# Turning the memory-gate rows by transfers through DRAM instead of TensorE transposes

## The chip, the cores and the metric

The kernel runs on one core of a Trainium2 chip. The metric is the device time of one execution in microseconds. The kernel before took 701.46 us in the median of three runs (700.98 to 701.46).

## The reference, cut to what matters

One layer of a streaming encoder, 512 tokens of 1024 channels, in float32. The normalised input goes through one wide projection (11,272 columns) that feeds two token mixers and two merge gates; the mixers' outputs are projected, merged, projected again and added to the input. The part that the change touches is the first mixer, a matrix memory with 4 heads. Two rows per head, an input gate and a forget gate, steer it:

```python
log_i = mi.transpose(0, 2, 1)                    # (B, heads, tokens)
log_f = jax.nn.log_sigmoid(mf).transpose(0, 2, 1)
bcum  = jnp.cumsum(fb, axis=-1)                  # per chunk
dmat  = bcum[..., :, None] - bcum[..., None, :] + ib[..., None, :]
m_t   = jnp.maximum(inter, jnp.max(dmat, axis=-1))
w_intra = jnp.exp(dmat - m_t[..., None])
h = num / jnp.maximum(jnp.abs(den), jnp.exp(-m_t))[..., None]
```

So every weight between a token t and an earlier token s is the exponential of (something of t) plus (something of s). The kernel works these out as a row over t, `rb`, and a column over s, `c`, with blocks of 128 tokens. Rows lie along one partition's free axis, columns along the partitions, and the numbers have to be had both ways.

## The kernel before, in words

The whole layer is a list of 110 units, numbered c. A unit is one block of weights (512 KB) with its 24 matmuls of 512 columns on TensorE (PE): each product is made three times, from a high and a low part of both operands (L85, L86, L87; the first four units have L1137 to L1139). A unit's weights are loaded by SP into one of three buffers `stg` (L110), split into `wh` on ScalarE (L90) and `wl` on VectorE (L91) up to two units ahead (AHEAD), and loaded up to four units ahead (LOADS); since there are three buffers, the load of the weights of one unit waits until the split three units earlier is through.

Beside the units run generators. The loop over c calls each active generator once per unit (not in the units in REST: 11, 16, 20, ...), and a `yield` ends its share of that unit. Instructions stand in each engine's queue in this order and engines work their queues in order, so what a generator issues in unit c stands behind the split for unit c+2 and ahead of that for unit c+3. The attention heads (from unit 10 on) send their blocks `ay` to `az` by 16 transfers per head on SP, in two halves (L458), and split `az` on ScalarE and VectorE a few units later. The four memory heads start in units 52, 56, 70 and 76.

The gates are one generator that starts in unit 4. The 4 heads' forget gates come out of TensorE as rows on partitions 32 to 35 (`g2`), the input gates on 0 to 3. Four transposes turn the forget rows into columns `f` of 128 partitions by 16 numbers (L546), where log-sigmoid is worked out; four transposes turn them back into rows (L570); two scans along the rows give `m` and `b` (L575, L581); `rb`, `c` and a copy of `rb` in two parts, `rb2`, follow (L583 to L587). Eight transposes and a product with ones then give `c_lag[0]`, `em` and `bs` as columns (L600 to L607), and `c_lag[1..3]` follow from them (L610). A memory head spreads its row of `rb` over the 128 partitions by one product with a selector `sel` (L706) and a copy out of the PSUM (L708); POOL masks the diagonal blocks into `w_all` (L713), and ScalarE takes the exponentials with `c_lag` as bias (L724).

Of the kernel before, what the change touches and what calls it, by code (L numbers as in the profile page):

```python
# [8 lines left out]
F32 = mybir.dt.float32  # L9
FR = mybir.dt.float32r  # L10
BF = mybir.dt.bfloat16
AF = mybir.ActivationFunctionType
OP = mybir.AluOpType

D = 1024
T = 512
KT = 8
TB = 4
# [16 lines left out]
def tile_hybrid_layer(  # L35
# [16 lines left out]
    nc = tc.nc  # L52
# [3 lines left out]
    def pool(name, bufs=1, **k):  # L56
        return ctx.enter_context(tc.tile_pool(name=name, bufs=bufs, **k))

    cst = pool("cst")
    hp = pool("hp")  # L60
    sp = pool("sp")
    mp = pool("mp")
    tiny = pool("tiny", 4)
    psd = pool("psd", 4, space=bass.MemoryType.PSUM)
    psa = pool("psa", 4, space=bass.MemoryType.PSUM)
    ctx.enter_context(tc.manual_schedule())
# [6 lines left out]
    def blk(tag, dt=F32, shape=(512,), name=None, p=128):  # L73

        where = mp if tag in MISC else sp
        return where.tile([p] + list(shape), dt, name=name or tag, tag=tag, bufs=BUFS[tag])
# [4 lines left out]
    def att_ps():  # L81
        return psa.tile([128, 512], F32, name="aps", tag="aps")
# [128 lines left out]
    ident = cst.tile([128, 128], F32, name="ident")  # L211
# [282 lines left out]


    NH = 4
    sel = cst.tile([128, NH, 128], FR, name="sel")
    rb2 = cst.tile([128, T], FR, name="rb2")
    c_lag = [cst.tile([128, TB, NH], F32, name=f"c_lag{k}") for k in range(TB)]
    em = cst.tile([128, TB, NH], F32, name="em")  # L500
    gst = blk("y", shape=(KT, 8), name="gst")

    wg_t = []

    def gates_fill():
        wg = blk("P5", FR, (KT, 128), name="wg")
        nc.gpsimd.memset(wg.bitcast(F32), 0.0)

        sel32 = blk("y", shape=(NH, 128), name="sel32", p=36)
        nc.gpsimd.memset(sel32, 1.0)  # L510
        for r in (slice(0, 4), slice(32, 36)):
            nc.gpsimd.affine_select(out=sel32[r], in_=sel32[r], compare_op=OP.is_equal, fill=0.0, base=0,
                                    channel_multiplier=1, pattern=[[-1, 4], [0, 128]])
        nc.gpsimd.memset(sel.bitcast(F32), 0.0)
        nc.gpsimd.memset(rb2.bitcast(F32), 0.0)
        wg_t.extend([wg, sel32])

    def gates_prep():
        wg, sel32 = wg_t
        for c in range(2):  # L520
            src = gst[:, :, 4 * c:4 * c + 4]
            nc.vector.tensor_copy(wg[:, :, 32 * c:32 * c + 4], src)
            nc.vector.tensor_tensor(wg[:, :, 64 + 32 * c:68 + 32 * c], src,
                                    wg[:, :, 32 * c:32 * c + 4].bitcast(F32), op=OP.subtract)
        nc.vector.tensor_copy(sel[0:4], sel32[0:4])
        nc.vector.tensor_copy(sel[32:36], sel32[32:36])

    def gates():
        def row(name, p=4):
            return blk("y", name=name, p=p)  # L530

        wg = wg_t[0]
        ps = att_ps()
        for k in range(KT):
            nc.tensor.matmul(ps, wg[:, k, :], hh[:, k, :], start=k == 0, stop=False)
            nc.tensor.matmul(ps, wg[:, k, :], hl[:, k, :], start=False, stop=k == KT - 1)
        g1 = row("g1", 36)
        nc.scalar.activation(g1, ps[64:100, :], AF.Copy)
        g2 = row("g2", 36)
        nc.vector.scalar_tensor_tensor(g2, ps[0:36, :], gbias, g1, op0=OP.add, op1=OP.add)  # L540
        gi = g2[0:4, :]
        yield

        fp = att_ps()
        for j in range(TB):
            nc.tensor.transpose(fp[:, 4 * j:4 * j + 4], g2[32:36, j * 128:(j + 1) * 128], ident[32:36, 32:36])  # L546

        def col(name):
            return tiny.tile([128, 16], F32, name=name, bufs=1)

        f, u, w, p = col("gf"), col("gu"), col("gw"), col("gp")
        nc.vector.tensor_copy(f, fp[:, 0:16])
        nc.scalar.activation(u, f, AF.Abs)
        nc.scalar.activation(u, u, AF.Exp, scale=-1.0)
        nc.scalar.activation(w, u, AF.Sigmoid)
        yield
        nc.vector.tensor_scalar(w, u, 2.0, None, op0=OP.add)
        nc.vector.reciprocal(w, w)
        nc.vector.tensor_tensor(u, u, w, op=OP.mult)
        nc.vector.tensor_tensor(w, u, u, op=OP.mult)  # L560
        nc.vector.tensor_scalar(p, w, 2.0 / 17, 2.0 / 15, op0=OP.mult, op1=OP.add)
        for c in (13, 11, 9, 7, 5, 3, 1):
            nc.vector.tensor_tensor(p, p, w, op=OP.mult)
            nc.vector.tensor_scalar(p, p, 2.0 / c, None, op0=OP.add)
        nc.vector.tensor_tensor(u, u, p, op=OP.mult)
        nc.vector.scalar_tensor_tensor(f, f, 0.0, u, op0=OP.min, op1=OP.subtract)
        yield
        lp = att_ps()
        for j in range(TB):
            nc.tensor.transpose(lp[0:4, j * 128:(j + 1) * 128], f[:, 4 * j:4 * j + 4], ident)  # L570
        f = row("gl")
        nc.vector.tensor_copy(f, lp[0:4, :])
        yield
        m = row("gm")
        nc.vector.tensor_tensor_scan(m, f, gi, 0.0, op0=OP.add, op1=OP.max)  # L575
        msk = row("gk")
        nc.vector.memset(msk, 1.0)
        nc.vector.memset(msk.rearrange("p (b t) -> p b t", b=TB)[:, :, 0:1], 0.0)
        b = row("gp")
        nc.vector.tensor_tensor_scan(b, msk, f, 0.0, op0=OP.mult, op1=OP.add)  # L580
        yield  # L581
        rb = row("gu")
        nc.vector.tensor_tensor(rb, b, m, op=OP.subtract)  # L583
        nc.vector.tensor_copy(rb2[0:4], rb)
        nc.vector.tensor_tensor(rb2[32:36], rb, rb2[0:4].bitcast(F32), op=OP.subtract)
        c = row("gw")
        nc.vector.tensor_tensor(c, gi, b, op=OP.subtract)  # L587
        ones4 = row("ones4")
        bend = ones4[:, 128:144].rearrange("p (x h) -> p x h", h=NH)
        ones4 = ones4[:, 0:128]  # L590
        for h in range(NH):
            nc.vector.tensor_scalar(bend[:, :, h:h + 1],
                                    b.rearrange("p (x t) -> p x t", x=TB)[:, :, 127:128],
                                    ident[0:4, h:h + 1], None, op0=OP.mult)
        nc.vector.memset(ones4, 1.0)
        yield
        tp = att_ps()
        for j in range(TB):
            js = slice(j * 128, (j + 1) * 128)
            nc.tensor.transpose(tp[:, 4 * j:4 * j + 4], c[:, js], ident[0:4, 0:4])  # L600
            nc.tensor.transpose(tp[:, 16 + 4 * j:20 + 4 * j], m[:, js], ident[0:4, 0:4])
        bb = att_ps()
        nc.tensor.matmul(bb[:, 0:16], ones4, bend.rearrange("p x h -> p (x h)"), start=True, stop=True)
        nc.vector.tensor_copy(c_lag[0], tp[:, 0:16].rearrange("p (j h) -> p j h", h=NH))
        nc.vector.tensor_copy(em, tp[:, 16:32].rearrange("p (j h) -> p j h", h=NH))
        bs = cst.tile([128, TB, NH], F32, name="bs")
        nc.vector.tensor_copy(bs, bb[:, 0:16].rearrange("p (j h) -> p j h", h=NH))  # L607
        for k in range(1, TB):
            n = TB - k
            nc.vector.tensor_tensor(c_lag[k][:, 0:n, :], c_lag[k - 1][:, 0:n, :],  # L610
                                    bs[:, k - 1:k - 1 + n, :], op=OP.add)
# [4 lines left out]
    class MPair:  # L616
# [84 lines left out]
        def head(self, h):  # L701
            hd = 2 * self.p + h
            qt = self.tr["q"][2 * h:2 * h + 2]
            kt = self.tr["k"][2 * h:2 * h + 2]
            rp = att_ps()
            nc.tensor.matmul(rp, sel[:, hd, :], rb2, start=True, stop=True)  # L706
            rbc = blk("om", shape=(516,))
            nc.vector.tensor_copy(rbc[:, 0:T], rp)  # L708
            w_all = blk("P5", shape=(1280,), name="w_all")
            for j in range(TB):  # L710
                lo = j * 128
# [2 lines left out]
                                        fill=-1e30, base=0, channel_multiplier=-1, pattern=[[1, 128]])  # L714
# [3 lines left out]
            for j in range(TB):  # L718
                lo = j * 128
                w = w_all[:, P_OFF[j]:P_OFF[j] + T - lo]  # L720
                for i in range(j, TB):
                    s = slice((i - j) * 128, (i - j + 1) * 128)
                    src = w[:, s] if i == j else rbc[:, i * 128:(i + 1) * 128]
# [74 lines left out]
            src = ht.rearrange("p (d a) i j -> p a d (i j)", d=2)  # L798
# [6 lines left out]
            for d in range(2):  # L805
                y = y_m[2 * hd + d].rearrange("p (i b j) -> p i b j", i=TB, b=4)
# [337 lines left out]

    later.setdefault(3, []).append(turn_vecs)
    later.setdefault(GATES_PREP, []).append(gates_prep)


    act = []
    pend = [(GATES_START, 1, lambda: True, gates)]  # L1150
    for s in (0, 1):
        for h in range(4):
# [30 lines left out]
    for c in range(N):  # L1183
# [17 lines left out]
        if c == 0:  # L1201
            x_scale(2)
            x_scale(3)
            gates_fill()
# [45 lines left out]
```

## Time and profile before

| | |
|---|---|
| median of three runs | 701.46 us (700.98 to 701.46) |
| the profiled execution's own time | 700.42 us |
| its span | 698.7 us |
| PE busy | 690.4 us, 99% |
| VectorE (DVE), ScalarE (ACT), GpSimd (POOL) busy | 463.5, 335.6, 109.2 us |
| mean busy share of the DMA engines, per 40th of the span | between 2 and 7 tenths |
| granted TensorE clock | full in every slice |

The span is what the trace covers; the execution's own time is 1.72 us longer. PE is the engine that is always at work, and the chain that ended last lies on it for 97% of the span. A busy PE says little by itself, since matmuls overlap and their ends are modelled; what a group of matmuls takes is read here from the starts of those around it. In steady stretches of 512-column products the starts lie 0.22 to 0.23 us apart.

### The profile page before, as it was taken

The page shows a single profiled execution, that of the slowest core. Times are in us where ns is not written, and L with a number is a line of the kernel's source. Part 1 is how long each engine was busy: PE and PEld are TensorE (multiplying, and loading weights), DVE is VectorE, ACT ScalarE, POOL GpSimd, SP SyncE. Part 2 cuts the span into 40 slices and gives each one's busy share as a digit, 9 for nine tenths or more (in the row PEclk, how much of TensorE's full clock was granted, in tenths as well). Part 3 has the DMA queues.
Part 4 walks back from the last instruction along what each step waited for, and adds up shares of the span by engine and source line. Part 5 has one row for each costly group of instructions (what it writes and reads, how often), then busy time and mean ns, then how long its engine had stood idle before and what let it go on. Part 6 is the DMA issues. An engine that isn't in the chain of part 4 may idle for free.

```text
span 698.7 us, 9267 instructions
## 1 busy us (share of the span) xinstructions
PE 690.4 (99%) x3220; PEld 575.2 (82%) x3220; DVE 463.5 (66%) x807; ACT 335.6 (48%) x629; POOL 109.2 (16%) x249
## 2 busy tenths in 40 slices
PE   7999999999999999999999999999999999999997
PEld 5888888888888888888888888888888888888876
DVE  6837887856787775389944738995343364445996
ACT  6245354475554543244475534446563353344451
POOL 5422122252130220000011120001111000111021
PEclk9999999999999999999999999999999999999999
DMA  7432424525433444333332244433323456589434
GB/s 247 136 106 71 126 63 123 148 59 145 112 107 84 130 109 137 90 95 94 97 98 67 61 108 120 120 90 91 91 61 86 112 157 219 144 184 208 126 81 130
DMA packets 104759, 80.94 MB, mean 116 GB/s; under 512 B 6766, under 2 KB 89096, under 8 KB 104712
## 3 DMA queue, kind: packets, MB, share of 16 engines
q1 hardware_dynamic: 102552, 74.45, 37.2%
q0 software_dynamic: 2016, 5.77, 4.5%
q8 instruction: 25, 0.41, 0.2%
q14 instruction: 22, 0.18, 0.1%
q10 hardware_dynamic: 144, 0.13, 0.1%
HBM read 65.12 MB, written 2.10 MB: 96 GB/s over the span
## 4 chain that ended last, share of the span: by engine, by line
PE 97%; DMA 1%; DVE 1%; POOL 0%; SPq 0%; issue 0%; ACT 0%; DVEq 0%
PE dps L85 27%; PE dps L86 27%; PE dps L87 27%; PE aps L86 3%; PE aps L87 3%; PE aps L85 3%; PE aps L389 1%; PE dps L1139 1%; PE dps L1137 1%; PE dps L1138 1%; DMA stg<-in_w_in_dram 1%; PE aps L760 1%; PE aps L762 1%; PE aps L761 1%; DVE fl L1096 0%; POOL fl L1096 0%
## 5 line engine op out<-in xcount | busy, mean ns | idle before, releaser
L91 DVE TENSOR_TENSOR wl<-stg,wh 128x1024 fp32r<-128x1024 f32 x92 | 112.6, 1223 | 112.9 <-ACT wh L90 111.3
L85 PE MATMUL dps<-hh,wh 128*128 128x512 f32 x448 | 175.2, 391 | 0.0
L87 PE MATMUL dps<-hh,wl 128*128 128x512 f32 x448 | 174.5, 389 | 0.0
L86 PE MATMUL dps<-hl,wh 128*128 128x512 f32 x448 | 174.5, 389 | 0.0
L90 ACT ACTIVATE wh<-stg 128x1024 fp32r<-128x1024 f32 x92 | 96.8, 1052 | 58.4 <-PE dps L87 38.2
L87 PEld LDWEIGHTS dps<-hh,wl 128*128 128x128 f32 x448 | 84.1, 188 | 17.8
L85 PEld LDWEIGHTS dps<-hh,wh 128*128 128x128 f32 x448 | 84.1, 188 | 17.1 <-DVE tmp L372 0.4
L86 PEld LDWEIGHTS dps<-hl,wh 128*128 128x128 f32 x448 | 84.2, 188 | 16.9
L85 PE MATMUL dps<-wh,hh 128*128 128x512 f32 x224 | 88.2, 394 | 0.1
L87 PE MATMUL dps<-wh,hl 128*128 128x512 f32 x224 | 87.3, 390 | 0.0
L86 PE MATMUL dps<-wl,hh 128*128 128x512 f32 x224 | 87.3, 390 | 0.0
L87 PEld LDWEIGHTS dps<-wh,hl 128*128 128x128 f32 x224 | 42.0, 188 | 9.0
L85 PEld LDWEIGHTS dps<-wh,hh 128*128 128x128 f32 x224 | 42.1, 188 | 8.6 <-issue 0.5
L86 PEld LDWEIGHTS dps<-wl,hh 128*128 128x128 f32 x224 | 42.1, 188 | 8.1
L651 DVE SCALAR_TENSOR_TENSOR acc<-tmp,vec,acc 128x511 f32<-128x511 f32 (+2 forms) x48 | 36.0, 750 | 1.7
L654 ACT ACTIVATE tmp<-acc 128x512 f32<-128x512 f32 x16 | 10.1, 633 | 50.8 <-DVE acc L651 50.8
L422 DVE TENSOR_TENSOR_SCAN om<-om 128x512 f32<-128x512 f32 (+3 forms) x32 | 26.7, 835 | 8.8 <-POOL om L416 8.8
L416 POOL TENSOR_SCALAR_AFFINE_SELECT om<-om 128x128 f32<-128x128 f32 x32 | 14.1, 441 | 109.0 <-ACT om L414 109.0
L713 POOL TENSOR_SCALAR_AFFINE_SELECT w_all<-om 128x128 f32<-128x128 f32 x16 | 6.0, 412 | 153.9 <-DVE om L708 136.8
L414 ACT ACTIVATE om<-aps,rq 128x512 f32<-128x512 f32 (+3 forms) x32 | 16.8, 525 | 22.8 <-PE aps L87 22.8
L85 PE MATMUL dps<-yh,wh 128*128 128x512 f32 x64 | 24.9, 389 | 0.0
L86 PE MATMUL dps<-yl,wh 128*128 128x512 f32 x64 | 24.9, 389 | 0.0
(271 smaller groups left out, 1225.3 us busy)
## 6 DMA issues: line engine op xcount, KB each, us to landing
stg<-in_w_in_dram SPq DMA_DIRECT2D x87, 512.0 KB, 3.8
az<-ay SPq DMA_DIRECT2D x128, 40.0 KB, 2.0
stg<-in_w_proj_s_dram SPq DMA_DIRECT2D x8, 512.0 KB, 3.7
B<-in_w_out_dram SPq DMA_DIRECT2D x8, 512.0 KB, 4.8
stg<-in_w_proj_m_dram SPq DMA_DIRECT2D x8, 512.0 KB, 3.6
wl<-stg POOLq DMA_DIRECT2D x8, 512.0 KB, 5.5
brow<-in_b_in_dram SPq DMA_DIRECT2D x8, 256.0 KB, 4.0
hz<-ht SPq DMA_DIRECT2D x64, 32.0 KB, 1.9
```

Source lines behind the costliest of these rows:

```text
L85: nc.tensor.matmul(ps, ah, bh, start=first, stop=False)
L86: nc.tensor.matmul(ps, ah, bl, start=False, stop=False)
L87: nc.tensor.matmul(ps, al, bh, start=False, stop=last)
L90: nc.scalar.activation(hi, src, AF.Copy)
L91: nc.vector.tensor_tensor(lo, src, hi.bitcast(F32), op=OP.subtract)
L389: nc.tensor.transpose(tp[:, tb * 128:(tb + 1) * 128], self.raw[name][tb][:, hs], ident)
L414: nc.scalar.activation(om[:, 0:n], zp, AF.Sigmoid, scale=rn[:, h:h + 1])
L416: nc.gpsimd.affine_select(out=om[:, ts], in_=om[:, ts], compare_op=OP.is_gt, fill=1.0, base=0, channel_multiplier=1, pattern=[[-1, 128]])
L422: nc.vector.tensor_tensor_scan(back, back, back, 1.0, op0=OP.mult, op1=OP.bypass)
L651: nc.vector.scalar_tensor_tensor(acc[:, j:], t[:, 0:T - j], cw(3 - j, ch), acc[:, j:], op0=OP.mult, op1=OP.add)
L654: nc.scalar.activation(t, acc, AF.Sigmoid)
L760: nc.tensor.matmul(nm[:, 0:258], ph, vh, start=j == 0, stop=False)
```

## The change

The transposes, the selector products and their PSUM copies go. In their place rows and columns are written to small DRAM tensors (`f_d`, `l_d`, `rb_d`, `c_d`, `m_d`, `b_d`: 8 KB each) and read back in the other order by transfers on SP. The new helper `by_token` reads a (4, 512) tensor back as 128 partitions by 4 numbers, 128 tokens at a time; each number is 4 bytes and its neighbours in the tile lie 2 KB apart in DRAM. A memory head reads its row of `rb_d` on all 128 partitions at once. The generator has four more `yield`s.

```diff
 def gates_fill():
-        sel32 = blk("y", shape=(NH, 128), name="sel32", p=36)
-        ... (memsets and selects of sel32, sel, rb2 on POOL)
 def gates_prep():
-        nc.vector.tensor_copy(sel[0:4], sel32[0:4])
-        nc.vector.tensor_copy(sel[32:36], sel32[32:36])
 def gates():
+        def by_token(dst, src):
+            for j in range(TB):
+                nc.sync.dma_start(dst[:, 4 * j:4 * j + 4],
+                                  src[:, j * 128:(j + 1) * 128].rearrange("h p -> p h"))
...
-        fp = att_ps()
-        for j in range(TB):
-            nc.tensor.transpose(fp[:, 4 * j:4 * j + 4], g2[32:36, j * 128:(j + 1) * 128], ident[32:36, 32:36])
-        nc.vector.tensor_copy(f, fp[:, 0:16])
+        f_d = dp.tile([NH, T], F32, name="f_d")
+        nc.sync.dma_start(f_d, g2[32:36, :])
+        yield
+        by_token(f, f_d)
+        yield
+        yield
...
-        lp = att_ps()
+        l_d = dp.tile([128, 16], F32, name="l_d")
+        nc.sync.dma_start(l_d, f)
+        yield
+        f = row("gl")
         for j in range(TB):
-            nc.tensor.transpose(lp[0:4, j * 128:(j + 1) * 128], f[:, 4 * j:4 * j + 4], ident)
-        f = row("gl")
-        nc.vector.tensor_copy(f, lp[0:4, :])
+            nc.sync.dma_start(f[:, j * 128:(j + 1) * 128], l_d[:, 4 * j:4 * j + 4].rearrange("p h -> h p"))
+        yield
         yield
...
-        nc.vector.tensor_copy(rb2[0:4], rb)
-        nc.vector.tensor_tensor(rb2[32:36], rb, rb2[0:4].bitcast(F32), op=OP.subtract)
+        nc.sync.dma_start(rb_d, rb)
...
-        (ones4 and bend: four products by ident's columns, a memset)
+        c_d, m_d, b_d = [dp.tile([NH, T], F32, name=n) for n in ("c_d", "m_d", "b_d")]
+        for d, src in ((c_d, c), (m_d, m), (b_d, b)):
+            nc.sync.dma_start(d, src)
         yield
-        tp = att_ps()
+        by_token(c_lag[0].rearrange("p j h -> p (j h)"), c_d)
+        by_token(em.rearrange("p j h -> p (j h)"), m_d)
+        bs = cst.tile([128, TB, NH], F32, name="bs")
         for j in range(TB):
-            nc.tensor.transpose(tp[:, 4 * j:4 * j + 4], c[:, js], ident[0:4, 0:4])
-            nc.tensor.transpose(tp[:, 16 + 4 * j:20 + 4 * j], m[:, js], ident[0:4, 0:4])
-        bb = att_ps()
-        nc.tensor.matmul(bb[:, 0:16], ones4, bend.rearrange("p x h -> p (x h)"), start=True, stop=True)
-        (three copies out of the PSUM)
+            nc.sync.dma_start(bs[:, j, :], bass.AP(tensor=b_d.tensor, offset=b_d.offset + 128 * j + 127,
+                                                   ap=[[0, 128], [T, NH]]))
+        yield
+        yield
...
 class MPair, def head(self, h):
-            rp = att_ps()
-            nc.tensor.matmul(rp, sel[:, hd, :], rb2, start=True, stop=True)
             rbc = blk("om", shape=(516,))
-            nc.vector.tensor_copy(rbc[:, 0:T], rp)
+            nc.sync.dma_start(rbc[:, 0:T], bass.AP(tensor=rb_d.tensor, offset=rb_d.offset + T * hd,
+                                                   ap=[[0, 128], [1, T]]))
```

On PE, where the first attention head's transposes (`qraw`, `kraw`) begin in unit 10, this stood before:

```order
L87 MATMUL dps<-wh,hl 128x512
L600 MATMUL aps<-ident,gw 128x4
L601 MATMUL aps<-ident,gm 128x4
L600 MATMUL aps<-ident,gw 128x4
L601 MATMUL aps<-ident,gm 128x4
L600 MATMUL aps<-ident,gw 128x4
L601 MATMUL aps<-ident,gm 128x4
L600 MATMUL aps<-ident,gw 128x4
L601 MATMUL aps<-ident,gm 128x4
L603 MATMUL aps<-ones_781 128x16
L389 MATMUL aps<-ident,qraw 128x128 x4
```

and this stands there now (the line numbers are one higher):

```order
L86 MATMUL dps<-wh,hh 128x512
L87 MATMUL dps<-wl,hh 128x512
L88 MATMUL dps<-wh,hl 128x512
L390 MATMUL aps<-ident,qraw 128x128 x4
L390 MATMUL aps<-ident,kraw 128x128 x4
```

The nine rows of the gates are gone. The four transposes of L546, the four of L570 and the four selector products of L706 leave PE's queue in the same way, and nothing else in it moves.

On SP, in the stretch of units 9 to 18, this stood before (`stg` are the weight loads, `brow` a bias row, `az` the attention heads' blocks):

```order
L110 DMA stg<-in_w_in_dram 128x8x128 x2
L304 DMA brow<-in_b_in_dram 128x512
L110 DMA stg<-in_w_in_dram 128x8x128 x2
L110 DMA stg<-in_w_in_dram 128x2x512 x4
L458 DMA az<-ay 32x320 x8
L110 DMA stg<-in_w_in_dram 128x2x512 x2
L458 DMA az<-ay 32x320 x8
L304 DMA brow<-in_b_in_dram 128x512
```

and from the second of these rows on this stands there now (`gl` are the turned forget rows, `c_lag`, `em` and `bs` the columns):

```order
L305 DMA brow<-in_b_in_dram 128x512
L111 DMA stg<-in_w_in_dram 128x8x128
L566 DMA l_d<-gf 128x16
L111 DMA stg<-in_w_in_dram 128x8x128
L111 DMA stg<-in_w_in_dram 128x2x512
L570 DMA gl<-l_d 4x128x1 x4
L111 DMA stg<-in_w_in_dram 128x2x512 x3
L583 DMA rb_d<-gu 4x512
L588 DMA c_d<-gw 4x512
L588 DMA m_d<-gm 4x512
L588 DMA b_d<-gp 4x512
L459 DMA az<-ay 32x320 x8
```

```order
L111 DMA stg<-in_w_in_dram 128x2x512 x2
L525 DMA c_lag_101<-c_d 128x4x1 x4
L525 DMA em<-m_d 128x4x1 x4
L594 DMA bs<-b_d 128x4x1 x4
L459 DMA az<-ay 32x320 x8
L305 DMA brow<-in_b_in_dram 128x512
```

The first half of the first head's `az` has moved behind four writes that wait for `gu` and `gw` of VectorE, and the second half behind twelve transfers of single numbers.

On VectorE the rows' scans leave the stretch of units 6 to 10 and stand now in unit 14 (in front of the attention head's `ay`), with `gu` and `gw` one unit on:

```order
L92 TENSOR_TENSOR wl<-stg,wh 128x1024
L574 SCALAR_TENSOR_TENSOR gm<-gl,g_508 4x512
L576 MEMSET gk 4x512
L577 MEMSET gk 4x4
L579 SCALAR_TENSOR_TENSOR gp<-gk,gl 4x512
L441 STREAM_TRANSPOSE ay<-a_all 128x4x32 x5
```

Before, the same scans stood behind the copy of `gl` out of the PSUM; now the first of them waits for four transfers.

## Rows read from the trace of the kernel before

**Rows 1.** The page's chain that ended last: shares of the span by engine.

```profile
PE 97%; DMA 1%; DVE 1%; POOL 0%; SPq 0%; issue 0%; ACT 0%; DVEq 0%
```

**Rows 2.** One stretch: length, busy PE, PEld, DVE, ACT, POOL, clock, DMA share, GB/s.

```profile
36.60:660.00 623.40, 623.34 (x2930) 522.51 (x2929) 404.25 (x700) 301.87 (x565) 85.80 (x210) 1.00 0.42 113
```

**Rows 3.** Timeline of PE around L546 and L570: start us, duration us, line.

```profile
48.41 0.39 PE L87 MATMUL dps<-wh,hl 128*128 128x512 f32 x1
...
49.41 0.40 PE L86 MATMUL dps<-wl,hh 128*128 128x512 f32 x1
...
59.85 0.39 PE L87 MATMUL dps<-wh,hl 128*128 128x512 f32 x1
...
60.75 0.39 PE L86 MATMUL dps<-wl,hh 128*128 128x512 f32 x1
```

**Rows 4.** Timeline of PE around L600 to L603, and at the second attention head.

```profile
76.64 0.39 PE L87 MATMUL dps<-wh,hl 128*128 128x512 f32 x1
...
77.78 0.33 PE L389 MATMUL aps<-ident,qraw 128*128 128x128 f32 x1
...
96.80 0.34 PE L87 MATMUL aps<-kth,qtl 128*128 128x384 f32 x1
96.97 0.60 PE L389 MATMUL aps<-ident,qraw 128*128 128x128 f32 x4
```

**Rows 5.** Timeline of PE at two of the four selector products.

```profile
350.61 0.39 PE L706 MATMUL aps<-rb,sel 128*128 128x512 f32 x1
350.84 0.40 PE L85 MATMUL dps<-hh,wh 128*128 128x512 f32 x1
...
370.96 0.44 PE L706 MATMUL aps<-rb,sel 128*128 128x512 f32 x1
371.24 0.40 PE L85 MATMUL dps<-hh,wh 128*128 128x512 f32 x1
```

**Rows 6.** Timeline of SP: issues in units 12 to 18, and in unit 52.

```profile
84.01 0.37 SPq L110 DMA_DIRECT2D stg<-in_w_in_dram  x1
...
116.97 5.28 SPq L458 DMA_DIRECT2D az<-ay  x8
...
122.98 0.37 SPq L110 DMA_DIRECT2D stg<-in_w_in_dram  x1
...
341.23 0.37 SPq L110 DMA_DIRECT2D stg<-in_w_in_dram  x1
```

**Rows 7.** Timelines of DVE, ACT and PE in the same units.

```profile
102.47 1.23 DVE L91 TENSOR_TENSOR wl<-stg,wh 128x1024 fp32r<-128x1024 f32 x1
...
109.30 1.22 DVE L91 TENSOR_TENSOR wl<-stg,wh 128x1024 fp32r<-128x1024 f32 x1 [0.20 <-ACT wh L90]
...
354.00 0.68 DVE L708 COPY om<-aps 128x512 f32<-128x512 f32 x1
...
133.77 1.03 ACT L90 ACTIVATE ath<-az 128x512 fp32r<-128x512 f32 x2
...
142.40 1.04 ACT L90 ACTIVATE wh<-stg 128x1024 fp32r<-128x1024 f32 x1
...
119.77 0.39 PE L85 MATMUL dps<-wh,hh 128*128 128x512 f32 x1
```

**Rows 8.** The page's DMA issues: KB each, median us to landing.

```profile
stg<-in_w_in_dram SPq DMA_DIRECT2D x87, 512.0 KB, 3.8
az<-ay SPq DMA_DIRECT2D x128, 40.0 KB, 2.0
...
brow<-in_b_in_dram SPq DMA_DIRECT2D x8, 256.0 KB, 4.0
```

**Rows 9.** The first 16 us by stretch, columns as in rows 2.

```profile
13.00:14.40 1.40, 1.30 (x10) 1.13 (x10) 1.40 (x2) 1.15 (x2) 1.40 (x2) 1.00 0.83 168
10.00:13.00 3.00, 2.09 (x10) 1.38 (x8) 2.46 (x8) 2.77 (x6) 2.54 (x5) 1.00 1.05 416
14.40:16.00 1.60, 1.24 (x5) 0.48 (x3) 1.60 (x2) 1.15 (x2) 1.52 (x2) 1.00 0.03 6
```

More of the change, by code (lines that the diff above doesn't have):

```diff
@@ L63, in tile_hybrid_layer @@
     tiny = pool("tiny", 4)
+    dp = pool("dp", space=bass.MemoryType.DRAM)
     psd = pool("psd", 4, space=bass.MemoryType.PSUM)
@@ L496, in tile_hybrid_layer @@
     NH = 4
-    sel = cst.tile([128, NH, 128], FR, name="sel")
-    rb2 = cst.tile([128, T], FR, name="rb2")
+    rb_d = dp.tile([NH, T], F32, name="rb_d")
     c_lag = [cst.tile([128, TB, NH], F32, name=f"c_lag{k}") for k in range(TB)]
@@ L507, in gates_fill @@
         nc.gpsimd.memset(wg.bitcast(F32), 0.0)
-        sel32 = blk("y", shape=(NH, 128), name="sel32", p=36)
[L510 to L516, printed above, removed]
+        wg_t.append(wg)
     def gates_prep():
-        wg, sel32 = wg_t
+        wg = wg_t[0]
         for c in range(2):
@@ L583, in gates @@
         nc.vector.tensor_tensor(rb, b, m, op=OP.subtract)
-        nc.vector.tensor_copy(rb2[0:4], rb)
-        nc.vector.tensor_tensor(rb2[32:36], rb, rb2[0:4].bitcast(F32), op=OP.subtract)
+        nc.sync.dma_start(rb_d, rb)
         c = row("gw")
         nc.vector.tensor_tensor(c, gi, b, op=OP.subtract)
[L588 to L595, printed above, removed]
+        c_d, m_d, b_d = [dp.tile([NH, T], F32, name=n) for n in ("c_d", "m_d", "b_d")]
+        for d, src in ((c_d, c), (m_d, m), (b_d, b)):
+            nc.sync.dma_start(d, src)
         yield
-        tp = att_ps()
+        by_token(c_lag[0].rearrange("p j h -> p (j h)"), c_d)
+        by_token(em.rearrange("p j h -> p (j h)"), m_d)
+        bs = cst.tile([128, TB, NH], F32, name="bs")
         for j in range(TB):
-            js = slice(j * 128, (j + 1) * 128)
-            nc.tensor.transpose(tp[:, 4 * j:4 * j + 4], c[:, js], ident[0:4, 0:4])
-            nc.tensor.transpose(tp[:, 16 + 4 * j:20 + 4 * j], m[:, js], ident[0:4, 0:4])
-        bb = att_ps()
-        nc.tensor.matmul(bb[:, 0:16], ones4, bend.rearrange("p x h -> p (x h)"), start=True, stop=True)
[L604 to L607, printed above, removed]
+            nc.sync.dma_start(bs[:, j, :], bass.AP(tensor=b_d.tensor, offset=b_d.offset + 128 * j + 127,
+                                                   ap=[[0, 128], [T, NH]]))
+        yield
+        yield
         for k in range(1, TB):
```

## The prediction, made before the changed kernel ran

> **What bounds the kernel now.** I read the chain of waits first: it lies on PE for 97% of the span [rows 1]. Then the busy times by stretch: from 36.60 to 660.00 us PE is at work in 623.34 of 623.40 us, with the clock granted in full (1.00, the 2.4 GHz level), while VectorE and ScalarE are busy for 404 and 302 us and the DMA engines for a mean of 0.42 [rows 2]. All the gate work and all four memory heads lie in that stretch. So a PE instruction taken out there ends everything behind it earlier by what it took of PE's queue, unless PE then waits; and a transfer or a VectorE operation put in or taken out is worth nothing until it makes PE wait. Two questions are left: what the removed PE instructions took, and whether the added transfers are late for anyone whom PE waits for.
>
> **What is removed from PE.** Matmuls overlap, so I don't add durations but compare starts. In a steady stretch one 512-column product follows the next after 0.23 us (350.61 to 350.84) [rows 5].
> - L546, four transposes: from the L87 ahead of them to the L86 behind the next L85 it is 49.41 - 48.41 = 1.00 us, where two steps of 0.23 would stand: 0.54 us.
> - L570, four transposes: 60.75 - 59.85 = 0.90, less 0.46: 0.44 us for both [rows 3].
> - L600 to L603, eight transposes and the product with ones: 77.78 - 76.64 = 1.14 us from an L87 to the first head's L389. Without them the step from a product to L389 remains; at the second head it is 0.17 us behind a product of 384 columns, and I take 0.23 behind one of 512: 0.91 us [rows 4].
> - L706, four products of 512 columns: the first takes 0.23 us to the next start, the second 371.24 - 370.96 = 0.28 [rows 5]. The heads of the second pair stand in the same places, so 2 x 0.23 + 2 x 0.28 = 1.02 us.
>
> Together 2.9 us. On VectorE some 6 us of copies, casts and small products go (the four copies L708 alone are 4 x 0.68 [rows 7]), and on POOL the fills at the start; I cost both at nothing, since PE doesn't wait for them in the stretch above.
>
> **What is added.** 30 transfers on SP: 6 writes of 8 KB, 20 reads of 512 single numbers each (four for `f`, four for `gl`, twelve for `c_lag`, `em`, `bs`), four reads of a row on 128 partitions. None of these kinds but the last is in the trace, so I bound three prices.
>
> *Issue on SP.* The eight issues of `az` take 5.28 us, 0.66 each; a weight load 0.37 [rows 6]. I take 0.6, with 0.37 and 1.3 (twice the dear one) as ends.
>
> *Moving the single numbers.* The nearest transfer is `gst`, 1024 runs of 32 bytes, 8 on each of 128 partitions. It is queued behind the first inputs and weights; from 10 to 13 us the engines move 416 GB/s, so it can't yet have had much of them, and from 14.40 on they are idle (0.03, 6 GB/s) [rows 9]. So its 1024 runs took at most 1.4 us beside the rest of the weights: on 16 engines 64 runs each, at most 22 ns a run, my estimate. I take 22 ns as the value for a 4-byte run too; below I allow half and, on the dear side, several times it, since a run that gathers 4 bytes 2 KB (or 64 bytes) from the last isn't shown. A read of 512 numbers on 16 engines then is 32 x 22 ns = 0.7 us; if only as many engines as there are outer rows work on it, `gl` with its 4 partitions has 128 x 22 ns = 2.8 us per transfer, 11.3 us for four.
>
> The Trainium skill says against this change, in "DMA: Bandwidth & Descriptors", section "Rules for kernel authors", that a strided last dimension lowers to one descriptor per element and should be rearranged; and in its section on why a DMA increments its semaphore by 16, that the number of engines is the largest up to 16 that divides the slowest dimension on both sides, which is 4 for `gl`. Its table of measured bandwidth has 10.5 ns for a small packet, and by it `gl` would take 5.4 us (an estimate). No run here shows these shapes yet; the sum does not change by it, since I bound `gl` at 4 engines anyway.
>
> *Landing.* 2.0 us for small ones (`az`), 4.0 for a row on 128 partitions (`brow`) [rows 8].
>
> **Who waits for them.** I follow the order of the changed program with these prices.
> - `f_d` and `f`: written in unit 5, read back in unit 6, first used in unit 8, two units or 2 x 24 x 0.23 = 11 us later. Hidden.
> - `gl`: SP issues it behind the load at 84.01, so from 84.4 to 86.8 us. Its first reader, the scan on VectorE, now stands behind the split that ends at 102.47 + 1.23 = 103.7 [rows 6, 7]. Of the 17 us after landing time, 2.8 or 11.3 us are used. Hidden; but what stands behind the scan on VectorE is the next splits, so this is the place where a dear price would begin to tell.
> - `rb_d`, `c_d`, `m_d`, `b_d` wait on SP for `gu` and `gw`, two row operations (about 0.68 us each, as the copy L708) behind the split that ends at 109.30 + 1.22 = 110.5. They go out until 114.3; behind them the first half of the first head's `az` (5.28 us, to 119.6), two loads (to 120.3), the twelve reads (7.2, to 127.5) and the second half of `az` (to 132.8, landing 134.8). Its reader on ScalarE ran at 133.77: 1 us late [rows 7]. The load of 122.98 now goes out at 133.8 and lands at 137.6, ahead of its split at 142.40 [rows 6 to 8]. The loads and the other heads' `az` behind it slide by some 10 us too, and less with each time that SP would have stood idle; as this load has 142.40 - 122.98 - 3.8 = 15.6 us to spare, I cost them at nothing. ScalarE is late by 1 us where a split is done 119.77 - 110.5 = 9 us before PE takes it [rows 7]: no cost on PE.
> - The twelve reads move 12 x 0.7 = 8.4 us of DMA work, at a mean share of 0.42: the loads beside them have the 9 us named.
> - `c_lag` is then whole at about 135 us; its first reader is ScalarE in unit 53, behind the copy of 354.00 [rows 7]. Hidden by over 200 us.
> - A memory head's row: SP meets it right behind the load at 341.23 and ahead of the next, so it lands at about 346, before the copy L708 at 354.00 that it replaces [rows 6 to 8]. Nothing is late; the four reads of 256 KB lie where the mean DMA share leaves more than half free [rows 2].
>
> So no wait reaches PE, and the sum is -2.9 us: 700.42 - 2.9 = 697.5 us for an execution like the profiled one. That one was 1.04 us below the median of the runs, so 701.46 - 2.9 = 698.6 us is my time.
>
> **Rivals.**
> - *Half the gain is lost in SP's queue.* If an issue costs 1.3 us, or each waits for one that lands late, the twelve reads take 15 us, `az` lands at about 143 and ScalarE stands for 9 us in front of it; the splits behind it use up their 9 us and PE waits some 1 to 2 us in units 21 to 24. Against it: of 128 issues of `az` eight take 5.28 us even where they come one behind the other. For it: SP is full there for 20 us. 700.1 us, within 0.2% of before, 14%.
> - *Slower, by single numbers that are dear.* `gl` on 4 engines has 512 runs on each. VectorE begins to wait from 17.3 us / 512 = 34 ns a run, and PE, after the 9 us that splits are ahead, from (17.3 + 9.2) / 512 = 52 ns. At 75 ns it is 38.4 - 26.5 = 12 us: 710 us. Weight loads of units 17 and 18 would be held up behind it on the same engines. For it: the shape isn't in the trace, and its outer side has only 4 rows. Against it: 22 ns is already an upper bound for runs eight times as long. 8%. The rules of the Trainium skill named above ("DMA: Bandwidth & Descriptors") would give the 4 engines, but its 10.5 ns not the price.
> - *It doesn't do what it says*: excluded for PE, whose order shows the 4 + 4 + 9 + 4 rows gone and nothing else moved.
> - *More than the sum*: the nine instructions of two shapes may also slow what follows them, up to 1 us: 697.3 us, 8%.
>
> **How the numbers follow.** The forecast has 70%, with 697.6 to 699.6 as its own range (0.5 us on the steps read from starts, 0.5 on the median). With it and the last rival, 78%, go nearly all of faster by over 0.2% (1.4 us, about what a measurement of this kernel can tell from no change): 0.77. Within 0.2% has 0.14, slower 0.09. The range of 8 in 10 takes in the first rival up to 700.9 and reaches down to 697.0.
>
> **What would show it.** In the changed trace PE's order around the first head's transposes should close to 0.23 us, units 53 and 73 should last as long as their neighbours, and PE should stay busy without a gap from 36 to 660 us. SP should issue `az` of the first head some 10 to 16 us later than now and be back in step by 150 us. The reads of 512 numbers should land in 2 to 4 us, `gl` in 5 to 13. I am wrong if VectorE waits at the first scan, or ScalarE at the first `ath`, for more than 9 us, and PE behind them; or if PE's starts don't close up where the rows are gone.

## The result, and the profile after

The changed kernel is a little slower, not faster: 701.66 us in the median of 20 runs (699.88 to 703.06) against 700.62 us for the kernel before, run beside it; the ratio is 1.0015, with a 95% interval from 1.0008 to 1.0022. Two of the 20 runs of the kernel before, at 864.5 and 1796.64 us, are in a slow state and don't count in the ratio. The profiled execution took 701.77 us, its span is 700.1 us, 1.4 us more than before.

The chain that ended last comes first. Where it lay on PE for 97% [rows 1], it now leaves PE for a stretch, and SP's queue (SPq), VectorE and ScalarE are in it:

```profile
PE 84%; SPq 3%; DVE 2%; ACT 1%; issue 0%; DMA 0%; DVEq 0%; POOL 0%; ACTq 0%
```

The stretch of [rows 2] says the same by its busy time: 2.65 us without a matmul, where it had been 0.06.

```profile
36.60:660.00 623.40, 620.75 (x2902) 520.44 (x2900) 396.81 (x678) 301.23 (x563) 85.26 (x210) 1.00 0.43 115
```

PE's own waits (engine, line waited for, us in total, times, longest) name two places in that stretch, the first and the last of these rows; all the others lie ahead of it, in the first 36 us:

```profile
PE dps L86 <- DVE qraw L336: 2.2, 1, 2.2
PE aps L294 <- DVE x L284: 1.7, 2, 0.9
...
PE aps L390 <- DVE kraw L356: 0.5, 1, 0.5
```

**The 2.2 us, followed back.** They fall on the first product of unit 20. PE's timeline (start us, duration us, line; in brackets the idle time and its releaser):

```profile
136.97 0.39 PE L87 MATMUL dps<-wl,hh 128*128 128x512 f32 x1
137.19 0.39 PE L88 MATMUL dps<-wh,hl 128*128 128x512 f32 x1
139.78 0.47 PE L86 MATMUL dps<-wh,hh 128*128 128x512 f32 x1 [2.19 <-DVE qraw L336]
```

The step to that product is 2.59 us. In the kernel before it was already longer than the usual 0.23 us, 139.16 - 138.71 = 0.45: PE waited 0.22 us there for the same copy, so this copy had no time to spare. The first of its four pieces starts 0.82 us ahead of PE's product before (138.34) and 0.83 us ahead after (138.95, below).

```profile
138.71 0.39 PE L87 MATMUL dps<-wh,hl 128*128 128x512 f32 x1
139.16 0.47 PE L85 MATMUL dps<-wh,hh 128*128 128x512 f32 x1
```

```profile
138.34 2.47 DVE L335 TENSOR_TENSOR qraw<-dps,brow 128x512 f32<-128x512 f32 x4
```

`qraw` L336 takes a finished block out of the PSUM bank `dps` that PE is to fill next. On VectorE it stands behind the split `atl` of the first head's `az`, and that waits for `ath` on ScalarE. First VectorE, then ScalarE:

```profile
132.38 1.23 DVE L92 TENSOR_TENSOR wl<-stg,wh 128x1024 fp32r<-128x1024 f32 x1 [0.96 <-ACT wh L91]
133.52 0.56 DVE L600 TENSOR_TENSOR c_lag<-c_lag,bs 128x12 f32<-128x12 f32 x3
135.65 1.16 DVE L92 TENSOR_TENSOR atl<-az,ath 128x512 fp32r<-128x512 f32 x2 [1.56 <-ACT ath L91]
136.73 1.08 DVE L441 STREAM_TRANSPOSE ay<-a_all 128x128 f32<-128x128 f32 x5
137.72 0.71 DVE L395 SCALAR_TENSOR_TENSOR qtl<-aps,qkw,qth 128x512 fp32r<-128x512 f32 x1
138.35 0.68 DVE L92 TENSOR_TENSOR ktl<-aps,kth 128x512 fp32r<-128x512 f32 x1
138.95 2.47 DVE L336 TENSOR_TENSOR qraw<-dps,brow 128x512 f32<-128x512 f32 x4
```

```profile
131.29 1.06 ACT L91 ACTIVATE wh<-stg 128x1024 fp32r<-128x1024 f32 x1 [1.70 <-PE dps L88]
134.99 1.05 ACT L91 ACTIVATE ath<-az 128x512 fp32r<-128x512 f32 x2 [2.64 <-DMA az<-ay]
```

ScalarE waits 2.64 us for `az`. It ran `ath` at 133.77 before, without a wait [rows 7]. The transfers come from SP's queue (`x8`: eight issues, the second number the time of all):

```profile
102.21 0.37 SPq L111 DMA_DIRECT2D stg<-in_w_in_dram  x1
111.33 0.28 SPq L583 DMA_DIRECT2D rb_d<-gu  x1
112.02 0.28 SPq L588 DMA_DIRECT2D c_d<-gw  x1
...
113.49 5.03 SPq L459 DMA_DIRECT2D az<-ay  x8
118.63 1.04 SPq L111 DMA_DIRECT2D stg<-in_w_in_dram  x2
119.72 2.15 SPq L525 DMA_DIRECT2D c_lag<-c_d  x4
121.92 3.38 SPq L525 DMA_DIRECT2D em<-m_d  x4
125.34 2.15 SPq L594 DMA_DIRECT2D bs<-b_d  x4
127.53 5.99 SPq L459 DMA_DIRECT2D az<-ay  x8
```

SP stands in front of the writes until `gu` and `gw` are there, issues the first half of `az`, two loads, the twelve reads (7.8 us) and only then the second half of `az`, at 127.53 instead of 116.97 [rows 6]. The chain of waits goes through just these: the writes, `az`, the reads, `az`, the landing, `ath`, `atl`, `ay`, `qtl`, `ktl`, `qraw`, PE. The last eight issues have one long one among them (shortest, median and longest in ns):

```profile
L459 SPq DMA_DIRECT2D az<-ay x8: 524/589/1617, 127.5 to 131.9; - x8
```

The sums `c_lag` (0.56 us), which the change put ahead of `atl` on VectorE, cost nothing here: they are through at 134.08, and `atl` waits for `ath` until 135.65.

**The clock behind the wait.** After the wait PE's steps go from 0.23 to 0.43 us. By stretch (columns as in [rows 2]; the clock is the last but two):

```profile
137.19:139.78 2.59, 0.40 (x3) 0.04 (x1) 2.59 (x8) 0.12 (x1) 0.00 (x0) 1.00 0.76 259
139.78:141.00 1.22, 1.22 (x5) 1.02 (x6) 1.22 (x3) 1.12 (x7) 0.00 (x0) 0.96 0.23 64
141.00:144.06 3.06, 3.06 (x8) 2.30 (x7) 0.42 (x1) 2.93 (x12) 2.22 (x5) 0.50 0.79 225
144.06:155.00 10.94, 10.94 (x52) 9.22 (x51) 4.96 (x6) 6.25 (x22) 6.98 (x14) 0.99 0.48 133
```

From 141.00 to 144.06 the granted clock is 0.50, the 1.2 GHz level; before that PE had been idle for 2.2 us. Unit 20 lasts 7.16 us instead of 5.53: another 1.63 us. (A unit's time is read here from the start of its first product to that of the next unit's.)

**The ledger of the profiled execution.** Units that became shorter: 5 by 0.56, 7 by 0.47, 10 by 0.20, 53 and 73 by 0.29 each, 56 and 76 by 0.26 each, together 2.33. Against it 2.59 - 0.45 = 2.14 of wait and 1.63 of half clock. -2.33 + 2.14 + 1.63 = +1.44 us; the span grew by 1.4. These are units 5 to 76; ahead of them PE is 0.29 us earlier than before, and behind its last product some 0.2 us come back.

**The 0.5 us at unit 10.** There PE waits for the scaling of `kraw`. On VectorE the log-sigmoid polynomial, 21 small operations from 71.56 to 75.99, now stands between that unit's split and the scaling:

```profile
70.41 1.23 DVE L92 TENSOR_TENSOR wl<-stg,wh 128x1024 fp32r<-128x1024 f32 x1 [3.42 <-ACT wh L91]
71.56 0.17 DVE L554 TENSOR_SCALAR gw<-gu 128x16 f32<-128x16 f32 x1
...
75.81 0.18 DVE L563 SCALAR_TENSOR_TENSOR gf<-gf,gu 128x16 f32<-128x16 f32 x1
75.90 1.65 DVE L356 TENSOR_SCALAR kraw<-kraw,rk 128x128 f32<-128x128 f32 x8
```

```profile
75.99 0.58 PE L390 MATMUL aps<-ident,kraw 128*128 128x128 f32 x3
77.03 0.33 PE L390 MATMUL aps<-ident,kraw 128*128 128x128 f32 x1 [0.46 <-DVE kraw L356]
77.11 0.48 PE L86 MATMUL dps<-wh,hh 128*128 128x512 f32 x1
```

### The profile page after: what moved, and what is told of

It is laid out like the page before. It is cut to its first block, busy times and chain, and to the rows that moved or that the text cites. A ratio compares the mean times of both kernels' runs of the same rounds, so it can differ in the third digit from the quotient of the medians.

```text
span 700.1 us, 9246 instructions
## 1 busy us (share of the span) xinstructions
PE 688.3 (98%) x3198; PEld 573.9 (82%) x3198; DVE 457.1 (65%) x789; ACT 335.3 (48%) x629; POOL 105.0 (15%) x244
## 4 chain that ended last, share of the span: by engine, by line
PE 84%; SPq 3%; DVE 2%; ACT 1%; issue 0%; DMA 0%; DVEq 0%; POOL 0%; ACTq 0%
PE dps L86 24%; PE dps L88 24%; PE dps L87 24%; PE aps L87 3%; PE aps L88 3%; PE aps L86 3%; SPq L459 1%; SPq L525 1%; PE aps L749 1%; PE aps L751 1%; PE aps L750 1%; PE aps L390 1%; DMA az<-ay 0%; DVE wl L92 0%; SPq L594 0%
## 5 line engine op out<-in xcount | busy, mean ns | idle before, releaser
L415 ACT ACTIVATE om<-aps,rq 128x512 f32<-128x512 f32 (+3 forms) x32 | 16.8, 525 | 24.4 <-PE aps L88 24.4
```

What stands on the lines that cost most here:

```text
L415: nc.scalar.activation(om[:, 0:n], zp, AF.Sigmoid, scale=rn[:, h:h + 1])
```

## Experiments

All are compared with the kernel before, run beside them (medians of 700.38 to 700.65 us). Theory: SP's queue brings `az` late and PE waits at unit 20. What the first four were to tell apart is which part of the added work does it.

**1. The twelve reads put off to unit 45.** They are not needed before unit 52.

```diff
+        while now[0] < 45:
+            yield
         by_token(c_lag[0].rearrange("p j h -> p (j h)"), c_d)
```

> The changed kernel with its twelve reads of c_lag, em and bs put off from unit 17 to unit 45. Theory (SP's queue makes the attention block az late, ScalarE waits for it, and with it the copies that free PE's banks at unit 20): the idle time of PE at unit 20 falls from 2.2 us to 0.2 or less, the clock stays full, and the gain of 2.9 us of the removed PE work shows: ratio to before 0.996, about 697.7 us where before has 700.6. Rival (VectorE is late at unit 20 because of its own added work there, the scans of unit 14 and gu and gw of unit 15): the wait stays above 1.5 us and the ratio stays at 1.000 to 1.002.

Measured: 698.34 us (5 runs), ratio 0.9969 [0.9957, 0.9981]. The second half of `az` goes out at 120.04, `ath` doesn't wait, and unit 20 starts in step, with a step of 0.46 us (0.45 before), at the full clock:

```profile
137.49 0.39 PE L88 MATMUL dps<-wh,hl 128*128 128x512 f32 x1
137.95 0.47 PE L86 MATMUL dps<-wh,hh 128*128 128x512 f32 x1
```

The 3.8 us of wait and half clock of the profiled execution are gone with the reads; SP is held for `gu` as in the change. The gain is 0.6 us short of the forecast, since unit 10 still loses its part. The `c_lag` sums, which need what the reads bring, went to unit 45 as well, so this run alone doesn't part the reads from the sums; experiments 2 and 3 do.

**2. Only the four reads of `em` put off to unit 45.**

> The changed kernel with only the four reads of em put off to unit 45 (3.4 us of SP's issues). Theory (SP's time in front of az): az's second half goes out 3.4 us earlier, ScalarE's wait of 2.6 us goes, PE's idle time at unit 20 falls to 0.2 us, the clock stays full: ratio 0.996, the same as with all twelve put off. Rival (the moving of the single numbers on the DMA engines holds az up): a third of it goes, PE still waits about 1.5 us, ratio 0.998 to 1.001.

Measured: 699.42 us (11 runs), 0.9984 [0.9975, 0.9992]. The theory is right on ScalarE and wrong on PE; the ratio falls into the rival's range, but not for its reason. `az` goes out at 125.88 and `ath` runs without a wait at 132.44, yet the step at unit 20 is 138.65 - 137.38 = 1.27 us. VectorE shows why: the `c_lag` sums, a small piece that the change moved here, and a short wait stand ahead of the copies:

```profile
132.57 1.23 DVE L92 TENSOR_TENSOR wl<-stg,wh 128x1024 fp32r<-128x1024 f32 x1 [0.96 <-ACT wh L91]
133.71 0.56 DVE L599 TENSOR_TENSOR c_lag<-c_lag,bs 128x12 f32<-128x12 f32 x3
134.51 1.16 DVE L92 TENSOR_TENSOR atl<-az,ath 128x512 fp32r<-128x512 f32 x2 [0.24 <-DMA brow<-in_b_in_dram]
```

1.27 - 0.45 = 0.82 is close to 0.56 + 0.24: what is late on VectorE reaches PE whole. (The row names `brow` for the 0.24 us, but `brow` landed only at 134.97; what they were stays open.) No half clock follows this wait.

**3. Twelve issues as in the change, but of 128 runs of 16 bytes each instead of 512 of 4 bytes** (contents not used; the true reads are made in unit 45).

```diff
...
+        for dst, d in ((c_lag[0], c_d), (em, m_d), (bs, b_d)):
+            for j in range(TB):
+                nc.sync.dma_start(dst[:, j, :], bass.AP(tensor=d.tensor, offset=d.offset + 4 * j,
+                                                        ap=[[16, 128], [1, NH]]))
+        while now[0] < 45:
+            yield
```

> The twelve true reads put off to unit 45 as in the kernel late_reads, and in their old place in unit 17 twelve reads of the same size and number as runs of 16 bytes (128 runs each in place of 512; what they bring is overwritten in unit 45). Theory (number of issues on SP): PE waits at unit 20 as in the changed kernel, 1.5 to 2.2 us, ratio 1.000 to 1.002. Rival (price of moving single numbers): the wait goes, ratio 0.996.

Measured: 699.24 us (12 runs), 0.9977 [0.9969, 0.9986], between the two forecasts. The issues take 6.3 us instead of 7.8, `az` goes out at 126.57, and PE still waits, less and at the full clock:

```profile
134.74 1.05 ACT L91 ACTIVATE ath<-az 128x512 fp32r<-128x512 f32 x2 [1.92 <-DMA brow<-in_b_in_dram]
```

```profile
139.53 0.47 PE L86 MATMUL dps<-wh,hh 128*128 128x512 f32 x1 [1.48 <-DVE qraw L336]
```

A quarter of the runs, moved in a quarter of the packets, still cost four fifths of the issue time, and it is the issues that keep `az` back: its third to fifth blocks are complete 1.9 us after their issue here and in the change alike, so by then the single numbers don't hold them up.

The wait of 1.92 us itself is not the issues' alone. In the trace a transfer of `az` ends with sixteen completion marks. Of the last block fifteen had come by 132.80, where `ath` was due at 132.82; the sixteenth came at 134.56. (The row names `brow`, which wasn't whole by then.) A 16 KB packet of instruction loading, in the page's queue q8, started at 132.18 and took 1.19 us; that it held the late mark up is likely but not shown, since the trace doesn't tell which DMA engine a mark comes from.

The trace of the change has such a packet too, at 131.72 for 1.43 us; behind it the sixth and seventh blocks of `az` have one late mark each (134.23 and 134.41) and the eighth issue takes the 1.62 us seen above. Without these `ath` would have started at about 134.0 and waited 1.6 us instead of 2.64, an estimate from 131.90 + 1.9 for the last block and the 0.19 us from its last mark to `ath`. Each trace here has a packet of this kind between 128.9 and 133.9; where `az` was complete by then, or `ath` due later (experiment 4: packet at 129.61, late mark at 131.74), it cost nothing.

The twelve runs fall into two groups, four from 697.82 to 698.25 us and eight from 699.01 to 700.45, as if the late mark came in some executions only; one was profiled, so this is inferred.

**4. The kernel before, with the twelve reads added in unit 17 and nothing removed** (and three writes behind `gu` and `gw`, where they don't hold SP).

> The kernel before, all its transposes and products kept, with the three writes of c, m and b and the twelve reads of c_lag, em and bs added (they bring the values that stand there already), the reads in unit 17. Theory (SP's queue is enough by itself): PE waits 1 to 2.5 us at unit 20, and if it stands long enough the clock falls behind it as in the changed kernel; ratio 1.002 to 1.006. Rival (it takes the moved gate work on VectorE as well): ratio 1.000.

Measured: 700.79 us (11 runs), 0.9999 [0.9991, 1.0008]. Here the theory that the reads alone suffice fell: `az` goes out at 124.08, 7.1 us late, and nobody waits.

```profile
105.00 5.04 SPq L459 DMA_DIRECT2D az<-ay  x8
110.80 6.37 SPq L111 DMA_DIRECT2D stg<-in_w_in_dram  x2
117.62 2.02 SPq L620 DMA_DIRECT2D c_lag<-c_d  x4
...
124.08 5.08 SPq L459 DMA_DIRECT2D az<-ay  x8
```

So the reads without the hold (4) and the hold without the reads (1) are both free, and the two together cost 3.8 us. (In 4 PE's gains are missing as well, so `ath` is due 1.7 us later than in the change.) The new theory: what counts is the sum of delays against one allowance.

**5. The hold removed, the reads kept, but one unit later:** the four writes go one unit behind `gu` and `gw`, and the reads with them.

```diff
-        nc.sync.dma_start(rb_d, rb)
         c = row("gw")
         nc.vector.tensor_tensor(c, gi, b, op=OP.subtract)
+        yield
+        nc.sync.dma_start(rb_d, rb)
```

> The changed kernel with the four writes of rb, c, m and bs one unit later than gu and gw, so that SP issues the first half of the first head's az without standing for gu; the twelve reads then come in unit 18. My theory (the hold of SP and the reads are both needed for the wait): no wait at unit 20 beyond 0.5 us; the kraw wait at unit 10 stays, so 698.3 us, ratio 0.997. Rival (twelve reads of single numbers ahead of the transfers of units 18 to 20 are enough by themselves): PE waits 1 us or more in units 20 to 22, ratio 0.999 to 1.002.

Measured: 698.1 us (7 runs), 0.9968 [0.9956, 0.9979], as forecast; step at unit 20: 139.23 - 138.78 = 0.45. In this order the twelve reads (126.98 to 135.88) stand behind the second half of `az` (120.86), not ahead of it. So the run shows that writes and reads placed there cost nothing; it doesn't part the hold from the reads, as the theory meant it to.

**6. Hold kept, three issues of 64-byte rows in the place of the twelve** (contents not used, true reads in unit 45).

> The changed kernel, but in unit 17 three reads of 64-byte rows (128 rows each, contents not used) stand in place of the twelve, and the twelve true reads are made in unit 45. SP is held for gu as before. My theory (the twelve issues, 7.8 us of SP's time, close the gap between the halves of az): three issues take about 1.8 us, the second half of az goes out at about 121.5 us, ScalarE doesn't wait, PE's step at unit 20 is 0.45 us and there is no stretch of half clock: as late reads, 698.3 us, ratio 0.997. Rival (single small runs on the DMA engines, or the hold for gu with anything behind it, delay az): a wait of 1 us or more at unit 20, ratio 0.999 to 1.002.

Measured: 697.86 us (5 runs), 0.9963 [0.9950, 0.9977]; `az` at 121.23, as expected, and 0.45 us at unit 20.

The allowance, from the rows of these traces (us; "due" is when ScalarE was free for `ath`, its start less its wait):

| kernel | second half of `az` goes out | `ath` due | between them | `ath` waits | step at unit 20 |
|---|---|---|---|---|---|
| before | 116.97 | 133.77 | 16.8 | 0 | 0.45 |
| free writes (5) | 120.86 | 133.84 | 13.0 | 0 | 0.45 |
| late reads (1) | 120.04 | 132.55 | 12.5 | 0 | 0.46 |
| three issues (6) | 121.23 | 132.28 | 11.1 | 0 | 0.45 |
| reads in before (4) | 124.08 | 134.01 | 9.9 | 0 | 0.45 |
| `em` late (2) | 125.88 | 132.44 | 6.6 | 0 | 1.27, VectorE |
| 16-byte runs (3) | 126.57 | 132.82 | 6.3 | 1.92, late mark | 1.86 |
| after | 127.53 | 132.35 | 4.8 | 2.64, late marks | 2.59 |

There is no wait of `ath` down to 6.6 us between the two, and there is one at 6.3 and 4.8, whatever shrank the time: SP's hold, its issues, or PE's own gains, which bring `ath` forward. Eight issues and the landing of the last took 132.15 - 125.88 = 6.3 us in (2), 134.56 - 126.57 = 8.0 in (3) and 134.80 - 127.53 = 7.3 in the change, the last two with the late marks told of under experiment 3.

**7. Polynomial, scans, writes and reads all one unit earlier** (one `yield` less behind `by_token(f, f_d)`), and **8. the same with the reads in unit 45.**

> The changed kernel with one unit less between f_d and the log-sigmoid polynomial: polynomial in unit 8, the two scans in unit 13, gu, gw and the four writes in unit 14, the twelve reads in unit 15, ahead of the first half of the first head's az instead of between its halves. My theory (PE's 2.2 us wait at unit 20 comes from SP held for gu and then by twelve reads, with VectorE's copies that free PE's banks standing behind az; and the 0.7 us at unit 10 from the polynomial ahead of the kraw scaling): SP is back in step before az, no wait at unit 20 beyond 0.5 us, none at unit 10, so about -3.0 us, 697.6 us, ratio 0.996. Rival: 7.8 us of reads ahead of az and of the weight loads make the splits late as well, or the polynomial meets another scaling in unit 8: a wait of 1 us or more moves to another place, ratio 0.997 to 1.000.

> As the kernel with the earlier polynomial, but the twelve reads are put off to unit 45. Both theories of the reads give no wait at unit 20. It tells the two waits apart: if the 0.7 us at unit 10 comes from the polynomial ahead of the kraw scaling, it is gone and the time is 0.7 us below that of the kernel with late reads alone (698.3): 697.6 us, ratio 0.996. If it comes from something else at unit 10 it stays: 698.3 us, 0.997.

Measured: 698.96 us (11 runs), 0.9976 [0.9968, 0.9985], and 699.07 us (12 runs), 0.9983 [0.9974, 0.9991]. The first lies in the rival's range, the second is above both of its forecasts. The theory was right on both waits: unit 10 takes 6.33 us in both (7.31 before, 7.11 after) and unit 20 starts in step. The rival was right that a wait would move: the scans had moved as well, into the unit where VectorE owes PE `ktl`. From 7 on VectorE and PE:

```profile
95.08 1.30 DVE L573 TENSOR_TENSOR_SCAN gm<-gl,g 4x512 f32<-4x512 f32 x1
...
97.07 1.21 DVE L578 TENSOR_TENSOR_SCAN gp<-gk,gl 4x512 f32<-4x512 f32 x1
...
102.47 0.68 DVE L92 TENSOR_TENSOR ktl<-aps,kth 128x512 fp32r<-128x512 f32 x1
```

```profile
101.65 0.39 PE L86 MATMUL aps<-kth,qth 128*128 128x512 f32 x1
103.21 0.50 PE L87 MATMUL aps<-ktl,qth 128*128 128x512 f32 x1 [1.17 <-DVE ktl L92]
```

Unit 14 takes 8.31 us (8.27 in 8) instead of 6.83, which gives back more than unit 10 had gained.

**9. Only the four selector products replaced, in the kernel before.**

> The kernel before with only the four selector products of the memory heads replaced by a read of rb's row on 128 partitions (and one write of rb). If the term of the four memory heads stands by itself, units 53, 56, 73 and 76 are each 0.26 to 0.29 us shorter: -1.1 us, 699.5 us, ratio 0.9984. Rival: the write of rb, which makes SP stand for gu ahead of the first half of az, costs PE a wait at unit 20 by itself: 1.000 or more.

Measured: 699.42 us (11 runs), 0.9986 [0.9978, 0.9995]; units 53, 56, 73 and 76 take 0.29, 0.26, 0.29 and 0.26 us less. The term stands by itself.

**10. The three moves together:** polynomial one unit earlier, scans where they are, writes one unit later, reads in unit 45.

```diff
         by_token(f, f_d)
         yield
-        yield
...
+        yield
         m = row("gm")
...
+        yield
+        nc.sync.dma_start(rb_d, rb)
...
+        while now[0] < 45:
+            yield
         by_token(c_lag[0].rearrange("p j h -> p (j h)"), c_d)
```

> The changed kernel with three steps moved: the polynomial one unit earlier (unit 8), the two scans left where they are (unit 14), the four writes one unit after gu and gw, the twelve reads in unit 45. My theory: no wait at units 10, 14 and 20, so the sum over the units is -0.56 (unit 5) -0.47 (unit 7) -0.98 (unit 10) -1.1 (53, 56, 73, 76) = -3.1 us against the kernel before: 697.3 us, ratio 0.9956. Rival: the waits seen at units 10 and 14 stand for work that VectorE has no room for, and another unit between 8 and 20 takes it: ratio 0.997 or more.

Measured: 697.58 us (5 runs), 0.9955 [0.9943, 0.9968], faster than both kernels. PE doesn't wait in the stretch (columns as in [rows 2]), and its chain is back at 97%:

```profile
36.60:657.00 620.40, 620.34 (x2908) 520.42 (x2907) 397.73 (x678) 301.30 (x562) 83.89 (x210) 1.00 0.42 115
```

## Why the prediction was wrong

The prediction forecast 2.9 us less; the kernel took 1 us more. From the median of twenty runs before, 700.62, its sum would give 697.7 us instead of 698.6, still further from the 701.66 measured.

*The step that failed* is "ScalarE is late by 1 us where a split is done 9 us before PE takes it: no cost on PE". Two things were wrong in it.

First, the lateness. The second half of `az` was forecast to go out at 127.5 and to land at 134.8; it went out at 127.53 and its reader started at 134.99. That the landing fits so well is partly luck: without the long issue and the late marks it would have been a microsecond earlier (estimate under experiment 3). But I compared it with the time at which `ath` ran before. Units 5, 7 and 10, 1.23 us shorter together, and the start-up, 0.29 us shorter in this execution, had brought PE, and with it ScalarE, forward, so `ath` was due at 132.35: 2.64 us late, not 1.

Second, and this decides, the allowance. I took the 9 us by which weight splits are ahead of PE as the allowance for everything on ScalarE and VectorE. Behind `ath` and `atl` on VectorE stand also the copies that empty PE's banks, and those had no time to spare: PE already waited 0.22 us for one of them in the kernel before. The step (138.71 to 139.16) stands in the trace of the kernel before, and the prediction has no term for it. Its sign of being wrong, a wait of more than 9 us at `ath`, rested on the same step: 2.64 us were enough. Experiment 2 shows it from the other side: 0.8 us on VectorE alone, with ScalarE in time, reach PE as 0.82 us.

*The half clock* was no term at all. 1.63 us of the loss in the profiled execution come from it. Among the twenty executions six have a mean granted clock of 1.000 and a median of 700.05 us, fourteen one of 0.997 or 0.998 and a median of 701.92. The difference, 1.87 us, is close to the 1.63 of the trace. Of the 68 runs of the kernel before beside the experiments, five have a mean clock of 0.998 or less. That the half clock lay in unit 20 in each of the fourteen is inferred, since one was profiled, and a low mean doesn't prove it: two of the five runs of experiment 1 have 0.997 and 0.998, and in the trace of experiment 5 (0.997) the half clock lies in the first 14 us.

*The term of L600 to L603* was right and hidden. Predicted 0.91 us, measured 0.20 in the change and 0.98 (7.31 - 6.33) once the polynomial stood a unit earlier (experiments 7, 8 and 10). I had followed what the added transfers make late and had not followed where the added `yield`s put VectorE's 21 small operations. (The change adds seven `yield`s, as its diff shows, not four; three of them stand ahead of these operations.)

*The other terms* were right: L546 0.54 forecast and 0.56 measured, L570 0.44 and 0.47, the selector products 1.02 and 1.10 (0.29 + 0.26 + 0.29 + 0.26). With all four the sum is 3.1 us, and experiment 10 shows it: its median lies 700.55 - 697.58 = 2.97 us below the kernel before.

*The added transfers.* The issues of the twelve reads took 0.5 us each, the dear one 1.7, against 0.6 assumed. The four of `gl` took 6.1 us together against 2.4; SP had time there. 4-byte packets took their engine 9 ns (the median of those on SP's queue), not 22; `gl` was hidden, as said: it had landed by 93.4, and the first scan ran at 102.10 without a wait. A memory head's row landed 3.9 us after its issue and nobody on PE waited for it. So the rival of dear single numbers fell.

*The first rival* had the mechanism: `az` behind the reads, ScalarE standing before it, PE waiting 1 to 2 us, and a result near the time of before. It asked for issues of 1.3 us or a wait of 9 us on ScalarE; neither happened. The allowance was smaller, not the delay larger: with nothing to spare in place of the 9 us, a wait of PE would have been a term of the sum.

The Trainium skill, "DMA: Bandwidth & Descriptors", section "Rules for kernel authors", also says that spreading DMAs over several issuing engines gives no bandwidth and only saves issue time on the sequencer. Issue time was what counted here (7.8 us on SP, in front of `az`); no run moved the reads to another engine's queue. The rule against strided last dimensions, weighed in the prediction, told of a cost that stayed hidden.

## What to carry to other kernels

An allowance belongs to one consumer: before calling a delay hidden, list everything that stands behind the delayed instruction on its engine, down to the PSUM copies that free PE's banks, and look for PE's longest steps, since a step of twice the usual length, as here, can mark a place with no slack. Measure lateness against the program after the change: when the bottleneck engine gains, everything that it waits for is due earlier. A transfer that is needed much later should be issued later too; and a `yield` put in to hide one wait moves all that follows it on every engine.

## What was unexpected of the hardware

A wait of PE of 2.2 us was followed by 3 us at the lower level of its clock (0.50 granted from 141.00 to 144.06), after 100 us of nearly unbroken work (from 36.60 on). The trace of experiment 5 has a second such place, in the start-up: PE waits 2.57 us for `hh`, and the granted clock is 0.50 from 11.00 to 14.00.

```profile
10.73 0.77 PE L1127 MATMUL dps<-fh,hh 128*128 128x512 f32 x1 [2.57 <-DVE hh L296]
```

```profile
11.00:14.00 3.00, 3.00 (x8) 2.40 (x8) 2.92 (x9) 2.77 (x6) 2.49 (x5) 0.50 0.95 317
```

The shorter waits seen here, 1.5 us in experiment 3 and 1.2 us in experiment 7, show no such stretch in their traces. Between experiment 3 and the change the price of a wait went from its own length to 1.8 times that (2.14 + 1.63 over 2.14). What decides it stays open: no run varied the length of the wait by itself.
